# An encoder step on one core: the first token block's output projection, split into mixer B's heads and mixer A's heads

## The chip, the core and the metric

One core of a Trainium2 chip runs the whole layer. The figure compared is device time in microseconds (us) for one execution. Three runs of the kernel before took 2215.9, 2210.39 and 2213.52 us. The profile is of a further execution, which took 2217.6 us.

The engines are named as in the profile: PE multiplies matrices (PEld loads its stationary operand), DVE, ACT and POOL work elementwise, SP issues the DMAs. Each takes its own instructions in the order in which they are written for it, and waits for the others through semaphores.

## The reference

```python
def layer(x, c, ...):
    h = adaln_in(x, gains[0], sh1, sc1)
    x = x + FFN_RES * g1[:, None] * rmsnorm(swiglu(h, w1_gate, w1_up, w1_down), gains[1])
    h = adaln_in(x, gains[2], sh2, sc2)
    qa, ka, va, qb, kb, vb = jnp.split(h @ w_in, SPLITS, axis=-1)
    ...
    oa, ob, rows = mixers(qa, ka, va, qb, kb, vb)
    o = jnp.concatenate([rmsnorm(oa, group_gains[:WIDTH_A]), rmsnorm(ob, group_gains[WIDTH_A:])], axis=-1) @ w_out
    x = x + g2[:, None] * rmsnorm(o, gains[3])
    h = adaln_in(x, gains[4], sh3, sc3)
    x = x + FFN_RES * g3[:, None] * rmsnorm(swiglu(h, w2_gate, w2_up, w2_down), gains[5])
    return x, rows
```

There are 1024 prompt tokens and 32 new tokens; the model is 1024 wide. Mixer A is banded attention with 8 heads of 64 over up to 640 keys for each 128 queries, mixer B a narrow window with 8 query heads. Their outputs are 512 wide each. Each half is normalised by itself (a group norm), the two are joined to 1024 columns and multiplied by `w_out`.

## The kernel before

**Token blocks.** Everything but attention runs over three blocks of tokens, numbered tb: 384, 384 and 288 wide. Activations stand transposed, so a block's array is 8 slices k of 128 channels by its tokens. `O[tb]` (named `o` in the profile) holds attention's output: slices 0 to 3 are mixer A's four pairs of heads, 4 to 7 mixer B's.

**Two-part products.** A projection is computed from a rounded part and a rest of each operand: `mm3` issues three matmuls for each slice (weight high by `hi`, weight high by `lo`, weight low by `hi`). Weights are loaded as 128x1024 pieces (`raw`) and split by one ACT copy (L303) and one DVE subtraction (L304) into `w`.

**Attention.** It is a list of 72 tiles, gone through by the loop over n from L1275 on. Pair p of heads and query block i make a tile; tiles 0 to 35 are mixer B's, 36 to 53 pairs 0 and 1 of mixer A, and 54 to 71 pairs 2 and 3 in alternation, each pair beginning with its tile of the new tokens. A tile forms scores `S` (PE), adds the bias and finds the maximum (DVE), exponentiates (ACT), scales, transposes through `pp` (PE) to `PT`, and multiplies by the values into `po`, which is copied to `O`. Scores of tile n+1 are issued while tile n is transposed. The query and key projections (`pq`) fill PE up to n = 53; after that there are none left.

**The group norm** (L1138) of block tb and half g (0 is mixer A, 1 mixer B) squares two pieces of 128x768 on ACT (`sq`), adds them up on POOL, sums over channels by matmuls with ones (`pss`), computes a reciprocal root in ten small DVE operations (`rv`, `rt`, `ry`), spreads it over partitions by matmuls (`pr`), copies it (`rstd`, ACT), multiplies (`z`, DVE), rounds (`o_hi`, ACT) and takes the rest (`o_lo`, POOL for the first of two pieces and DVE for the second). It is a generator: `begin` puts it in a list of side work, `step` advances the first of that list by one piece, and `need` advances until one of them is finished.

**The order before.** At n = 55 (`GN1`) the mixer B norms of all three blocks begin. Mixer A's norm of a block begins two tiles after that block's last tile: n = 63 for block 0, n = 69 for block 1, and after the loop for block 2. `out_piece` (L1164) makes 128 output columns m of one block: 24 matmuls `wo`, then an ACT copy into `fo`. `OUTS` places five of block 0's eight pieces in the loop, one each at n = 67 to 71. The other three, then eight of block 1 (m from 7 down) and eight of block 2, follow the loop, with six side steps behind each. `KEEP` holds the weights of columns 5 to 7 from block 0 for block 1, so `w_out` is loaded in 13 pieces. After a block's last piece, its residual and next norm begin as side work (`h3`), which the second feed-forward (`gate`, `up`, `dn`) needs.

**Buffers.** 384-wide arrays of all kinds share six buffers (tag u): two are `O[0]` and `O[1]`, and the others hold the projections' inputs until n = 53. Scratch of 128x768 (`sq`, `z`, `PT` and others) shares five (tag h), raw weights three, split weights eight.

The program's order per engine comes from the framework's own scheduler, which moves instructions ahead of others where its estimate says that they are ready; so the written order is a priority, and the orders shown below are what was built.

Of the kernel before, what the change touches and what calls it, by code (L numbers as in the profile page):

```python
# [16 lines left out]
D = 1024  # L17
# [20 lines left out]
OUTSTEP = 6  # L38
ABREAST = 1
POOL_ADDS = (1, 2)  # L40
GN1 = 55
SC = (1, 3)
SCB = 1
JN = (1, 3)
# [21 lines left out]
PREP = 3  # L66
STAGES = ((0, 34), (37, 54))
RATE = 1.0
OUTS = (0,) * 13 + (1,) * 5
LAG = 0.5  # L70
KEEP = [(5, 6, 7), None, None]


@with_exitstack
def encoder_step(ctx: ExitStack, tc, x_prompt, x_sample, cache_a_k, cache_a_v, cache_b_k, cache_b_v,
# [30 lines left out]
    def s_tile(shape, name, dt=F32):  # L106
        return spool.tile(shape, dt, name=name, tag="s")
# [386 lines left out]
    def begin(key, gen, first=False):  # L494
        side.insert(0 if first else len(side), marked(key, gen))
# [641 lines left out]

    def group_norm(tb, g):  # L1138
        w = TB[tb][1]
        if OH[tb] is None:  # L1140
            OH[tb] = (u_tile(tb, "o_hi", F32R), u_tile(tb, "o_lo", F32R))
        hi, lo = OH[tb]
        pr = yield from mean_rstd(O[tb], range(4 * g, 4 * g + 4), w, 2.0 / D, JG, p1)
        r = s_tile([128, 384], "rstd")
        ae.activation(r[:, :w], pr[:, :w], AF.Copy)
        for c in range(2):
            z = h_tile([128, 2, 384], "z")
            for q in range(2):
                k = 4 * g + 2 * c + q
                ve.scalar_tensor_tensor(z[:, q, :w], O[tb][:, k, :], cst[:, 120 + k:121 + k], r[:, :w],  # L1150
                                        op0=OP.mult, op1=OP.mult)
            yield
            s = slice(4 * g + 2 * c, 4 * g + 2 * c + 2)
            ae.activation(hi[:, s, :], z[:, :, :w], AF.Copy)
            (ge if c in GNP else ve).tensor_tensor(lo[:, s, :], z[:, :, :w], hi[:, s, :], op=OP.subtract)
            yield

    wo, F2 = {}, [None] * 3
    outs = [(0, m) for m in range(KT)] + [(1, m) for m in reversed(range(KT))] + [(2, m) for m in range(KT)]

    def load_wo(m):
        wo[m] = split_cols(w_out, m)

    def out_piece():  # L1164
        tb, m = outs.pop(0)
# [67 lines left out]
    with tc.manual_schedule(engines={mybir.EngineType.PE}) if MANUAL else ExitStack():  # L1233
# [6 lines left out]
        for n in range(N):  # L1240
            for first, last, units in flows:
                if n == first:
                    now = now if PRIME == 2 and n == 0 else flow(units)
                    rate = sum(COST[key[0]] for key, _, _ in units) / (last - first) / 2 * RATE
            if n == GN1:
                for tb in range(3):
                    begin(("gn", tb, 1), group_norm(tb, 1))
            for tb in range(2):
                if n == whole[tb] + 2:
                    begin(("gn", tb, 0), group_norm(tb, 0), first=True)  # L1250
            for _ in range(OUTS[n - 54] if n >= 54 else 0):
                if outs and n >= whole[outs[0][0]] + 2:
                    out_piece()
            for key in opens.get(n + PREP, []):
                while key not in ready:
                    budget -= next(now, 0)
                preps.append(prepare(*key))
            for half in range(2):
                scores(n, half)
                tiles[n].tr(half)  # L1260
                if half == 0 and n:
                    tiles[n - 1].av()
                step(1)
                prep_step()
                fill(rate)
            for _, last, _ in flows:
                if n == last - 1:
                    fill(1e6)
                    budget = 0.0
    tiles[N - 1].av()  # L1270
    begin(("gn", 2, 0), group_norm(2, 0), first=True)
    while outs:
        out_piece()
# [82 lines left out]
```

## Time and profile before

| | |
|---|---|
| runs | 2215.9, 2210.39, 2213.52 us (median 2213.52) |
| profiled execution | 2217.6 us, of which the span from first to last instruction is 2215.8 us |
| DVE busy | 1239.1 us (56%) |
| ACT busy | 697.8 us (31%) |
| POOL busy | 179.2 us (8%) |
| mean granted PE clock | 0.984 |

A row of a window gives its start and end in us from the first instruction, its length, the busy time of each engine with the number of instructions, the granted share of PE's clock, the DMA engines' busy share and GB/s. A row of the timeline gives start, length, engine, line, operation and its operands; in brackets stands the engine's idle time before it and what ended it. PE's busy time is a model: matmuls overlap, so a start-to-start distance says more than a length.

### The profile page before, as it was taken

How to read it: one execution, taken by the hardware profiler on the slowest of the kernel's cores; microseconds unless marked ns; L12 is line 12 of the kernel's file. 1: busy time of each engine (PE TensorE's matmuls, PEld its weight loads, DVE VectorE, ACT ScalarE, POOL GpSimd, SP SyncE). 2: the span in 40 equal slices, each digit the busy share in tenths (PEclk: the TensorE clock that was granted, in tenths of full speed). 3: DMA queues.
4: the chain of work that ended last, by engine and by line, in shares of the span. 5: the costliest groups of instructions: out<-in, count | busy, mean ns of one | idle time of the engine just before them, and what ended most of it. 6: DMA issues, size and time to landing. Idle time of an engine off the chain costs nothing.

```text
span 2215.8 us, 33976 instructions
## 1 busy us (share of the span) xinstructions
PE 2161.6 (98%) x14012; PEld 2068.6 (93%) x14012; DVE 1239.1 (56%) x2425; ACT 697.8 (31%) x1450; POOL 179.2 (8%) x281
## 2 busy tenths in 40 slices
PE   6999999999999999899999899999999999999998
PEld 4999999999999999799787589999999999999998
DVE  5788667874333497677444865785333333333336
ACT  4411111111121253576444663542111111111133
POOL 1100000000000023001110313220000000000000
PEclk8999999999999999899999899999999999999999
DMA  9253334434122352111112121424211111111122
GB/s 323 93 153 118 111 96 124 143 101 129 39 66 69 101 184 93 38 39 30 50 30 62 46 77 67 134 86 120 66 58 39 57 39 39 58 38 58 39 69 79
DMA packets 200623, 186.03 MB, mean 84 GB/s; under 512 B 7597, under 2 KB 169813, under 8 KB 199317
## 3 DMA queue, kind: packets, MB, share of 16 engines
q1 hardware_dynamic: 200468, 183.87, 27.1%
q8 instruction: 110, 1.80, 0.3%
q14 instruction: 45, 0.36, 0.1%
HBM read 164.12 MB, written 22.86 MB: 84 GB/s over the span
## 4 chain that ended last, share of the span: by engine, by line
PE 90%; DVE 4%; DMA 3%; ACT 1%; issue 1%; POOL 0%; SPq 0%; ACTq 0%; DVEq 0%; POOLq 0%
PE dn L325 7%; PE dn L326 7%; PE dn L327 7%; PE gate L327 7%; PE gate L326 7%; PE up L327 7%; PE up L326 7%; PE gate L325 7%; PE up L325 7%; PE po L713 3%; PE S L752 2%; PE pq L325 2%; PE pq L327 2%; PE pq L326 2%; DMA raw<-in_w_gate_dram 1%; PE pp L776 1%
## 5 line engine op out<-in xcount | busy, mean ns | idle before, releaser
L326 PE MATMUL gate<-h_lo,w 128*128 128x384 f32 (+1 forms) x1056 | 340.2, 322 | 4.0 <-DVE h_lo L446 4.0
L325 PE MATMUL dn<-gg,w 128*128 128x384 f32 (+1 forms) x1056 | 341.4, 325 | 1.1 <-DVE facc L581 1.0
L581 DVE TENSOR_TENSOR facc<-dn,facc 128x768 f32<-128x768 f32 (+1 forms) x240 | 212.9, 889 | 230.2 <-PE dn L327 229.9
L326 PE MATMUL dn<-gg,w 128*128 128x384 f32 (+1 forms) x1056 | 340.6, 323 | 0.6 <-DVE gg L554 0.6
L325 PE MATMUL gate<-h_hi,w 128*128 128x384 f32 (+1 forms) x1056 | 341.0, 323 | 0.0
L327 PE MATMUL gate<-h_hi,w 128*128 128x384 f32 (+1 forms) x1056 | 340.4, 322 | 0.0
L325 PE MATMUL up<-h_hi,w 128*128 128x384 f32 (+1 forms) x1056 | 340.2, 322 | 0.0
L326 PE MATMUL up<-h_lo,w 128*128 128x384 f32 (+1 forms) x1056 | 340.0, 322 | 0.0
L327 PE MATMUL dn<-gg,w 128*128 128x384 f32 (+1 forms) x1056 | 340.0, 322 | 0.0
L327 PE MATMUL up<-h_hi,w 128*128 128x384 f32 (+1 forms) x1056 | 339.9, 322 | 0.0
L304 DVE TENSOR_TENSOR w<-raw,w 128x1024 fp32r<-128x1024 f32 x187 | 231.5, 1246 | 150.5 <-ACT w L303 150.3
L303 ACT ACTIVATE w<-raw 128x1024 fp32r<-128x1024 f32 x187 | 195.7, 1056 | 266.1 <-PE dn L327 103.5
L550 ACT ACTIVATE sl<-gate 128x384 f32<-128x384 f32 (+1 forms) x132 | 60.9, 462 | 563.9 <-PE gate L327 560.9
L551 DVE TENSOR_TENSOR sl<-sl,up 128x384 f32<-128x384 f32 (+1 forms) x132 | 68.5, 519 | 292.1 <-PE up L327 286.1
L326 PEld LDWEIGHTS gate<-h_lo,w 128*128 128x128 f32 x1056 | 198.6, 188 | 4.6 <-DVE h_lo L446 4.6
L325 PEld LDWEIGHTS dn<-gg,w 128*128 128x128 f32 x1056 | 199.2, 189 | 1.6 <-DVE facc L581 1.2
L326 PEld LDWEIGHTS dn<-gg,w 128*128 128x128 f32 x1056 | 199.2, 189 | 1.0 <-DVE gg L554 0.9
L327 PEld LDWEIGHTS dn<-gg,w 128*128 128x128 f32 x1056 | 199.1, 189 | 0.0
L325 PEld LDWEIGHTS gate<-h_hi,w 128*128 128x128 f32 x1056 | 198.7, 188 | 0.1
L327 PEld LDWEIGHTS gate<-h_hi,w 128*128 128x128 f32 x1056 | 198.7, 188 | 0.0
L327 PEld LDWEIGHTS up<-h_hi,w 128*128 128x128 f32 x1056 | 198.7, 188 | 0.0
L325 PEld LDWEIGHTS up<-h_hi,w 128*128 128x128 f32 x1056 | 198.5, 188 | 0.0
(224 smaller groups left out, 3367.4 us busy)
## 6 DMA issues: line engine op xcount, KB each, us to landing
raw<-in_w_mod_dram SPq DMA_DIRECT2D x56, 512.0 KB, 4.0
raw<-in_w_gate_dram SPq DMA_DIRECT2D x54, 512.0 KB, 4.0
raw<-in_w_up_dram SPq DMA_DIRECT2D x54, 512.0 KB, 4.7
raw<-in_w_down_dram SPq DMA_DIRECT2D x54, 512.0 KB, 4.5
raw<-in_w_in_dram SPq DMA_DIRECT2D x18, 512.0 KB, 4.3
wm<-in_w_mod_dram SPq DMA_DIRECT2D x8, 1024.0 KB, 7.4
raw<-in_w_out_dram SPq DMA_DIRECT2D x13, 512.0 KB, 4.5
xr<-xs SPq DMA_DIRECT2D x16, 384.0 KB, 3.5
```

The lines of the kernel that those rows point to most:

```text
L303: ae.activation(w[:, 0], r, AF.Copy)
L304: ve.tensor_sub(w[:, 1], r, w[:, 0])
L325: te.matmul(ps, w[:, 0, k], hi, start=start, stop=False)
L326: te.matmul(ps, w[:, 0, k], lo, start=False, stop=False)
L327: te.matmul(ps, w[:, 1, k], hi, start=False, stop=stop)
L550: ae.activation(sl[:, :w], ps[0][:, :w], AF.Silu)
L551: ve.tensor_tensor(sl[:, :w], sl[:, :w], ps[1][:, :w], op=OP.mult)
L581: ve.tensor_tensor(o, ps[:, :, :w], o, op=OP.add)
L713: te.matmul(po[64 * h:64 * h + 64, :n], vsl(j, h, kn), PT(h, j, kn), start=j == 0, stop=j == nt - 1)
L752: te.matmul(S[:, c:ce], self.T[:, h, :], KQ[:, 0, 128 * k0 + c:128 * k0 + ce], start=True, stop=True)
L776: te.transpose(pp[:, j - j0, :], P[:, 128 * j:128 * j + 128], ident)
```

## The change

Block 0's output projection is no longer made by `out_piece`. Each of its eight columns is made in two halves of the sum over channels: `half_piece` issues 12 matmuls over mixer B's four slices and copies the sum to `fo` (ACT); a later one issues 12 over mixer A's four slices and adds the sum to `fo` (DVE). The mixer B halves stand at n = 55 to 59, 61, 63 and 65; the mixer A halves at n = 66, 67 (one each) and 68 to 70 (two each). All of block 0 is so inside the loop, and after the loop 16 pieces follow where there were 19.

Each half loads its own weights, 512 rows by 256 columns for two halves: 8 pieces. Nothing is kept for block 1, which loads 8 pieces: 16 in all.

The norms move too. Block 0's mixer B norm begins at n = 51 and is finished by n = 54. The mixer B norms of blocks 2 and 1 begin at n = 65, in that order. A norm now asks for its output arrays after its reciprocal root and no longer before it.

```diff
-GN1 = 55
+GN1 = (51, 65)
+EARLY = (55, 56, 57, 58, 59, 61, 63, 65)
+LATE = 66
...
-OUTS = (0,) * 13 + (1,) * 5
...
-KEEP = [(5, 6, 7), None, None]
+KEEP = [None, None, None]
...
     def group_norm(tb, g):
         w = TB[tb][1]
+        pr = yield from mean_rstd(O[tb], range(4 * g, 4 * g + 4), w, 2.0 / D, JG, p1)
+        r = s_tile([128, 384], "rstd")
+        ae.activation(r[:, :w], pr[:, :w], AF.Copy)
         if OH[tb] is None:
             OH[tb] = (u_tile(tb, "o_hi", F32R), u_tile(tb, "o_lo", F32R))
         hi, lo = OH[tb]
-        pr = yield from mean_rstd(O[tb], range(4 * g, 4 * g + 4), w, 2.0 / D, JG, p1)
-        r = s_tile([128, 384], "rstd")
-        ae.activation(r[:, :w], pr[:, :w], AF.Copy)
...
-    outs = [(0, m) for m in range(KT)] + [(1, m) for m in reversed(range(KT))] + [(2, m) for m in range(KT)]
+    outs = [(1, m) for m in reversed(range(KT))] + [(2, m) for m in range(KT)]
...
+    halves = [(1, m) for m in range(KT)] + [(0, m) for m in range(KT)]
+    wh = {}
+
+    def load_half(g, j):
+
+        if (g, j) not in wh:
+            r = rpool.tile([128, 4, 256], F32, name="raw", tag="r")
+            dma.dma_start(r, w_out[0, 512 * g:512 * g + 512, 256 * j:256 * j + 256]
+                          .rearrange("(k p) n -> p k n", p=128))
+            w = wh[g, j] = wpool.tile([128, 2, 4, 256], F32R, name="w", tag="w")
+            ae.activation(w[:, 0], r, AF.Copy)
+            ve.tensor_sub(w[:, 1], r, w[:, 0])
+
+    def half_piece():
+
+        g, m = halves.pop(0)
+        need(("gn", 0, g))
+        if F2[0] is None:
+            F2[0] = u_tile(0, "fo", F32)
+        load_half(g, m // 2)
+        if m % 2 and halves:
+            load_half(halves[0][0], halves[0][1] // 2)
+        w, c0 = wh[g, m // 2], 128 * (m % 2)
+        hi, lo = OH[0]
+        ps = p1("wo")
+        for kk in range(4):
+            k = 4 * g + kk
+            wa, wb = w[:, 0, kk, c0:c0 + 128], w[:, 1, kk, c0:c0 + 128]
+            te.matmul(ps[:, :384], wa, hi[:, k, :], start=kk == 0, stop=False)
+            te.matmul(ps[:, :384], wb, hi[:, k, :], start=False, stop=False)
+            te.matmul(ps[:, :384], wa, lo[:, k, :], start=False, stop=kk == 3)
+        o = F2[0][:, m, :]
+        if g:
+            ae.activation(o, ps[:, :384], AF.Copy)
+        else:
+            ve.tensor_tensor(o, ps[:, :384], o, op=OP.add)
+        if m % 2:
+            del wh[g, m // 2]
+        if not halves:
+            begin(("h3", 0), between(F2[0], 0, 1, H3))
...
-            if n == GN1:
-                for tb in range(3):
-                    begin(("gn", tb, 1), group_norm(tb, 1))
+            if n == GN1[0]:
+                begin(("gn", 0, 1), group_norm(0, 1))
+            if n == GN1[1]:
+                begin(("gn", 2, 1), group_norm(2, 1))
+                begin(("gn", 1, 1), group_norm(1, 1))
...
-            for _ in range(OUTS[n - 54] if n >= 54 else 0):
-                if outs and n >= whole[outs[0][0]] + 2:
-                    out_piece()
+            if n == EARLY[0] - 1:
+                need(("gn", 0, 1))
+                load_half(1, 0)
...
                 fill(rate)
+                if half == 0 and n in EARLY:
+                    half_piece()
+                if n >= LATE and halves and (n + half) % 2 * (n < LATE + 2) == 0:
+                    half_piece()
...
     tiles[N - 1].av()
+    while halves:
+        half_piece()
+        step(2)
     begin(("gn", 2, 0), group_norm(2, 0), first=True)
```

**PE, at the start of the last two pairs.** Before, from the transposes of pair 3's tile of the new tokens (`pps`) on; the number behind a name tells tiles of one name apart:

```order
L902 MATMUL pps_11917<-ident_96,Ps_11872 128x64 x4
L903 MATMUL pps_11917<-ident_96,Ps_11872 32x64
L713 MATMUL po_11926<-PTs_11887,aux_11656 64x32 x8
L713 MATMUL po_11926<-PTs_11887,vs_9149 64x32 x2
L752 MATMUL S_12006<-KQ_11278,qz_11912 128x128
L776 MATMUL pp_11974<-ident_96,P_11908 128x128
L713 MATMUL po_11977<-PTs_11923,aux_11656 64x32 x8
L713 MATMUL po_11977<-PTs_11923,vs_9149 64x32 x2
L752 MATMUL S_12020<-KQ_10777,qz_11968 128x256
```

In the change, from the end of the first half piece to the start of the second:

```order
L1193 MATMUL wo_11987<-o_hi_11884,w_11908 128x384
L1194 MATMUL wo_11987<-o_hi_11884,w_11908 128x384
L1195 MATMUL wo_11987<-o_lo_11885,w_11908 128x384
L777 MATMUL pp_12027<-ident_96,P_11956 128x128
L753 MATMUL S_12061<-KQ_11278,qz_11960 128x128
L753 MATMUL S_12075<-KQ_10777,qz_12021 128x256
L714 MATMUL po_12030<-PTs_11971,aux_11660 64x32 x8
L714 MATMUL po_12030<-PTs_11971,vs_9149 64x32 x2
L1193 MATMUL wo_12047<-o_hi_11884,w_11908 128x384
L1194 MATMUL wo_12047<-o_hi_11884,w_11908 128x384
L1195 MATMUL wo_12047<-o_lo_11885,w_11908 128x384
```

Twelve `wo` matmuls in one run now stand between the scores and transposes of successive tiles.

**PE, at the end of the loop.** Before, the last matmul of attention (`po_13068`) stands among the pieces of block 0; from it to `pss_13111`, the sum of block 2's mixer A norm, are 19 `wo` of block 0's sixth piece, and behind `pr_13138` of that norm the seventh begins:

```order
L326 MATMUL wo_13085<-o_lo_11939,w_13082 128x384
L327 MATMUL wo_13085<-o_hi_11938,w_13082 128x384
L357 MATMUL pss_13111<-ones_98,sq_13115 128x1 x2
L357 MATMUL pss_13111<-ones_98,sq_13115 32x1
L405 MATMUL pr_13138<-ident_96,ry_13126 128x128 x2
L405 MATMUL pr_13138<-ident_96,ry_13126 128x32
L325 MATMUL wo_13147<-o_hi_11938,w_13144 128x384
L326 MATMUL wo_13147<-o_lo_11939,w_13144 128x384
```

In the change, from the last matmul of attention (`po_13159`) on; `pss_13171` and `pr_13198` belong to block 2's mixer A norm, `pss_13242` and `pr_13267` to block 1's mixer B norm, and `wo_13293` is block 1's first piece:

```order
L714 MATMUL po_13159<-PT_13145,vt_9148 64x128
L358 MATMUL pss_13171<-ones_98,sq_13175 128x1 x2
L358 MATMUL pss_13171<-ones_98,sq_13175 32x1
L406 MATMUL pr_13198<-ident_96,ry_13186 128x128 x2
L406 MATMUL pr_13198<-ident_96,ry_13186 128x32
L358 MATMUL pss_13242<-ones_98,sq_13246 128x1 x3
L406 MATMUL pr_13267<-ident_96,ry_13255 128x128 x3
L326 MATMUL wo_13293<-o_hi_13218,w_13290 128x384
L327 MATMUL wo_13293<-o_lo_13219,w_13290 128x384
```

No projection stands between attention's last matmul and the two norms any more.

**DVE, at the same place.** Before, from the last step of block 2's mixer A root on (`o_8219` is block 2's `O`, `o_8218` block 1's); the row behind these is the root of block 2's mixer B norm:

```order
L338 SCALAR_TENSOR_TENSOR ry_13126<-rt_13127,ry_13126 128x3
L1150 SCALAR_TENSOR_TENSOR z_13175<-o_8219,cst_110,rstd_13173 128x288 x2
L1150 SCALAR_TENSOR_TENSOR z_13180<-o_8219,cst_110,rstd_13173 128x288 x2
L1150 SCALAR_TENSOR_TENSOR z_13187<-o_8218,cst_110,rstd_13185 128x384 x2
L1150 SCALAR_TENSOR_TENSOR z_13223<-o_8218,cst_110,rstd_13185 128x384 x2
L1155 TENSOR_TENSOR o_lo_12792<-z_13180,o_hi_12791 128x576
L1155 TENSOR_TENSOR o_lo_12181<-z_13223,o_hi_12180 128x768
```

In the change, from the same step to the start of the root of block 1's mixer B norm (`rv_13253`):

```order
L339 SCALAR_TENSOR_TENSOR ry_13186<-rt_13187,ry_13186 128x3
L1151 SCALAR_TENSOR_TENSOR z_13206<-o_8219,cst_110,rstd_13202 128x288 x2
L1151 SCALAR_TENSOR_TENSOR z_13211<-o_8219,cst_110,rstd_13202 128x288 x2
L1151 SCALAR_TENSOR_TENSOR z_13220<-o_8218,cst_110,rstd_13216 128x384 x2
L1151 SCALAR_TENSOR_TENSOR z_13225<-o_8218,cst_110,rstd_13216 128x384 x2
L1151 SCALAR_TENSOR_TENSOR z_13232<-o_8219,cst_110,rstd_13230 128x288 x2
L1156 TENSOR_TENSOR o_lo_13205<-z_13211,o_hi_13204 128x576
L1151 SCALAR_TENSOR_TENSOR z_13237<-o_8219,cst_110,rstd_13230 128x288 x2
L1156 TENSOR_TENSOR o_lo_13219<-z_13225,o_hi_13218 128x768
L1156 TENSOR_TENSOR o_lo_13205<-z_13237,o_hi_13204 128x576
L392 TENSOR_SCALAR rv_13253<-pss_13242 128x3
```

Block 2's mixer B norm has moved in front of block 1's, whose whole chain now stands behind the loop. The square of block 1's mixer B half on ACT (`sq_13243`) stands behind the `o_hi` of `z_13232`, and POOL's additions of it behind three `o_lo`.

## The prediction

> **What bounds the kernel.** I read the page first, then windows over the stage around the change, then the timeline inside each window.
>
> ```profile
> PE 2161.6 (98%) x14012; PEld 2068.6 (93%) x14012; DVE 1239.1 (56%) x2425; ACT 697.8 (31%) x1450; POOL 179.2 (8%) x281
> PE 90%; DVE 4%; DMA 3%; ACT 1%; issue 1%; POOL 0%; SPq 0%; ACTq 0%; DVEq 0%; POOLq 0%
> ```
>
> PE is the bound, and the change removes no matmul of it. It can win only where PE lacks work or runs at a lower clock, and lose where its work leaves a gap uncovered. Three windows hold the places: from the last two pairs' start to the first exponential of tile 64, from there to the end of attention's last matmul, and 33 us behind it. The columns are PE, PEld, DVE, ACT, POOL, granted clock, DMA share and GB/s.
>
> ```profile
> 1213.00:1258.70 45.70, 39.36 (x235) 24.36 (x232) 36.56 (x105) 30.50 (x79) 19.14 (x51) 0.81 0.30 84
> 1258.70:1328.80 70.10, 69.44 (x495) 55.18 (x493) 49.77 (x125) 49.05 (x97) 14.67 (x22) 1.00 0.21 61
> 1328.80:1361.50 32.70, 29.53 (x158) 28.34 (x159) 19.64 (x42) 12.95 (x22) 13.75 (x10) 0.90 0.06 17
> ```
>
> In the first, PE idles 45.70 - 39.36 = 6.3 us, and a clock of 0.81 takes another 0.19 x 45.70 = 8.7 us. Short waits for softmax make it, such as
>
> ```profile
> 1224.83 0.33 PE L776 MATMUL pp<-ident,P 128*128 128x128 f32 x1 [1.48 <-ACT P L764]
> 1242.21 0.90 PE L776 MATMUL pp<-ident,P 128*128 128x128 f32 x3 [1.17 <-DVE P L766]
> ```
>
> The third holds the end of attention. PE's rows there:
>
> ```profile
> 1328.35 0.43 PE L713 MATMUL po<-PT,vt 128*64 128x128 f32 x2
> ...
> 1331.97 0.34 PE L327 MATMUL wo<-o_hi,w 128*128 128x384 f32 x1
> 1332.89 0.76 PE L357 MATMUL pss<-ones,sq 128*128 128x1 f32 x6 [0.58 <-POOL sq L370]
> 1336.01 1.76 PE L405 MATMUL pr<-ident,ry 128*128 128x128 f32 x6 [2.36 <-DVE ry L338]
> 1337.70 0.69 PE L325 MATMUL wo<-o_hi,w 128*128 128x384 f32 x1
> ...
> 1338.51 0.52 PE L327 MATMUL wo<-o_hi,w 128*128 128x384 f32 x1
> 1338.83 0.52 PE L325 MATMUL wo<-o_hi,w 128*128 128x384 f32 x1
> ...
> 1341.50 0.33 PE L325 MATMUL wo<-o_hi,w 128*128 128x384 f32 x1
> 1341.67 0.34 PE L326 MATMUL wo<-o_lo,w 128*128 128x384 f32 x1
> ```
>
> Attention's last matmul ends at 1328.8. PE then has 19 `wo` and two short waits, 2.9 us together. A `wo` starts 0.17 us after the one ahead at full clock (1341.50 to 1341.67) and 0.32 us at the low one (1338.51 to 1338.83), which lasts from 1337.7 to about 1341.
>
> **The change, part by part.** All sums use 0.174 us per `wo` at full clock.
>
> *Inside the loop.* Of the eight mixer B halves seven stand ahead of tile 64: 7 x 12 x 0.174 = 14.6 us into the first window, which has 6.3 + 8.7 = 15.0 us to spare, scattered in pieces shorter than a half's 2.1 us. PE takes them in written order, so a score or transpose behind a half waits for it, and DVE and ACT behind that score. In the second window the `wo` become fewer: nine halves, 108 matmuls, for
>
> ```profile
> 1258.70:1328.80 70.10, 23.66 (x126) 21.54 (x126) 2.45 (x5) 1.00 0.21 61
> ```
>
> so 18 x 0.174 = 3.1 us leave. DVE gains eight additions from PSUM and the loop three more weight splits; the nearest rows are
>
> ```profile
> L304 DVE TENSOR_TENSOR w<-raw,w 128x1024 fp32r<-128x1024 f32 x187 | 231.5, 1246 | 150.5 <-ACT w L303 150.3
> L303 ACT ACTIVATE w<-raw 128x1024 fp32r<-128x1024 f32 x187 | 195.7, 1056 | 266.1 <-PE dn L327 103.5
> L551 DVE TENSOR_TENSOR sl<-sl,up 128x384 f32<-128x384 f32 (+1 forms) x132 | 68.5, 519 | 292.1 <-PE up L327 286.1
> ```
>
> which makes 8 x 0.519 + 3 x 1.246 = 7.9 us on DVE and 3.2 on ACT. DVE was busy 36.56 + 49.77 = 86.3 of 115.8 us, 75%, and one norm's multiplications leave the loop, so most of this hides. Three more DMAs of 512 KB hide too (DMA share 0.30 and 0.21). The new order of the three matmuls of a product costs nothing, since every matmul has its own load already (14012 of each). Forcing block 0's mixer A norm at n = 66 puts its latency in front of a half; what PE waits for it has no row, and I leave it inside the bounds. Bounds: all idle time and the 3.1 us won, -9.4; all new DVE work exposed, +7.9. I take **-4**, on the gain's side because no engine but PE is above 75%.
>
> *At the loop's end.* This speaks against the change. Of block 0, 19 + 48 = 67 `wo` used to follow attention's last matmul; now none do, and block 1's first piece stands behind `pr` of two norms, one behind the other: block 2's mixer A, which needs attention's last output, and block 1's mixer B, whose operations DVE, ACT and POOL take behind those of three other norms. Queued behind that `pr` on PE are all 16 remaining pieces. The chain before, on the other engines:
>
> ```profile
> 1329.00 1.05 ACT L303 ACTIVATE w<-raw 128x1024 fp32r<-128x1024 f32 x1
> 1329.94 0.68 ACT L364 ACTIVATE sq<-o 128x576 f32<-128x576 f32 x1
> 1330.70 1.27 POOL L368 TENSOR_TENSOR sq<-sq 128x288 f32<-128x288 f32 x1 [3.23 <-ACT sq L364]
> 1337.81 0.79 ACT L1145 ACTIVATE rstd<-pr 128x288 f32<-128x288 f32 x2 [4.97 <-PE pr L405]
> 1338.25 5.09 DVE L1150 SCALAR_TENSOR_TENSOR z<-o,cst,rstd 128x288 f32<-128x288 f32 x8 [2.38 <-ACT rstd L1145]
> 1343.24 2.47 POOL L1155 TENSOR_TENSOR o_lo<-z,o_hi 128x768 fp32r<-128x768 f32 x1 [1.37 <-ACT o_hi L1154]
> 1354.39 2.31 ACT L364 ACTIVATE sq<-fo 128x768 f32<-128x768 f32 x3
> ```
>
> The changed order puts the same eight `z` at the same distance from attention's end, to 1343.3. What DVE and POOL do then, by form in the same stretch:
>
> ```profile
> L1150 DVE SCALAR_TENSOR_TENSOR z<-o,cst,rstd 128x288 f32<-128x288 f32 x8 | 5.1, 706 | 5.8 <-ACT rstd L1145 5.8
> L1155 POOL TENSOR_TENSOR o_lo<-z,o_hi 128x576 fp32r<-128x576 f32 x2 | 3.6, 1808 | 7.2 <-ACT o_hi L1154 7.2
> L1155 DVE TENSOR_TENSOR o_lo<-z,o_hi 128x576 fp32r<-128x576 f32 x2 | 2.7, 1365 | 0.0
> L368 POOL TENSOR_TENSOR sq<-sq 128x384 f32<-128x384 f32 x2 | 2.2, 1142 | 7.2 <-ACT sq L364 7.2
> L1155 DVE TENSOR_TENSOR o_lo<-z,o_hi 128x768 fp32r<-128x768 f32 x1 | 2.0, 2021 | 0.5 <-ACT o_hi L1154 0.5
> L1154 ACT ACTIVATE o_hi<-z 128x768 fp32r<-128x768 f32 x2 | 1.7, 840 | 1.5 <-DVE z L1150 1.5
> L370 POOL TENSOR_TENSOR sq<-sq 128x384 f32<-128x384 f32 x1 | 1.1, 1116 | 0.1
> ```
>
> DVE: four `z` (2.8), `o_lo` twice of 576 (2.7) and once of 768 (2.0), 7.6 us, to 1350.9. POOL: from its `o_lo`'s end at 1345.7 one more (1.8) and three additions (3.4), also to 1350.9. From a `pss` to the `wo` behind its `pr` took 4.8 us (1332.89 to 1337.70): PE restarts at 1355.7. Twelve `wo` over mixer A's slices at the low clock take 3.8 us; the next need mixer B's `o_hi`, behind a `rstd` and three squares on ACT (about 0.5 + 2.3 + 0.8 us, to 1359.4), and `o_lo` on POOL (2.5): 1361.9. The kernel before has by 1361.5 done
>
> ```profile
> 1328.80:1361.50 32.70, 25.69 (x134) 24.73 (x135) 2.41 (x5) 0.90 0.06 17
> ```
>
> 134 `wo`, 67 of which the change no longer owes. Of the other 67 the change has done 13. So it is 54 x 0.174 = 9.4 us behind, with the 0.4 us of the restart 9.8. If POOL and DVE did not slow each other (I allow 2 us), `pr` and the twelve `wo` ran at full clock (0.8 and 1.7), the restart would come 4.5 us earlier: +5.3. I take **+8**, near the rows of the same place. Behind the stall the low clock may last as it did before, ten `wo` at 0.15 us more: 0 to 1.5, I take **+0.7**. [...]
>
> *At the second feed-forward's start* block 1's norm is late:
>
> ```profile
> 1430.00:1450.00 20.00, 17.25 (x87) 16.78 (x86) 16.64 (x36) 8.51 (x15) 4.64 (x6) 0.83 0.10 35
> 1442.92 0.45 PE L326 MATMUL gate<-h_lo,w 128*128 128x384 f32 x1 [2.13 <-DVE h_lo L446]
> ```
>
> 2.75 us idle and 0.17 x 20 = 3.4 us of clock are lost. Block 0's residual and norm, which share DVE and ACT with block 1's, now come 28 `wo` (4.9 us) earlier against block 1's pieces (85 stand ahead of the residual's `pr`, and 113 did). Bounds -4.9 and +1 (a fifth of that, should DVE be late from the stall); I take **-2.5**.
>
> **The sum**: -4 + 8 + 0.7 - 2.5 = +2.2 us on the profiled execution's 2217.6 (span 2215.8), so 2219.8. That execution lies 4.1 us above the median of the runs, 2213.5; for the median the forecast is **2215.7 us**.
>
> **Rivals.**
>
> 1. *The stall is not paid back, slower.* If the halves delay scores as much as they fill, the loop keeps its length (0), the stall costs its upper 9.8, the clock 1.5, and the feed-forward gains nothing: +11.3, 2224.8 us. Its place is `pr` of block 1's mixer B norm. It decides as soon as the loop wins less than about 4 us. For it: every step of the chain has a row. Against: DVE and ACT have a quarter of the loop free.
> 2. *The loop shortens, faster.* The first window keeps its full clock and its waits are filled: -9.4, with +5.3, 0 and -4.9 for the rest: -9.0, 2204.5 us. For it: PE's loads are busy only 24.36 of 45.70 us there, so the busy 39.36 may hold waiting; the halves would then have 21.3 us to lie in. Against: the scores wait behind each half. [...]
> 3. *The halves don't fill the early gaps*, because weights or norm come late. The first `w_out` split was at 1217.1 (the row below), ahead of where the first half stands, so I give it little: the first two halves, 4.2 us, exposed, 2219.9 us.
>
> ```profile
> 1217.14 1.06 ACT L303 ACTIVATE w<-raw 128x1024 fp32r<-128x1024 f32 x1 [0.73 <-DMA raw<-in_w_out_dram]
> ```
>
> **How the numbers follow.** The likeliest case, a gain in the loop given back at its end, has 0.42 with its own range of 2208 to 2220; rival 1 has 0.30, rival 2 0.25 and rival 3 0.03. A measurement tells 0.3%, 6.6 us, from no change: faster lies below 2206.9 and slower above 2220.2. Rival 2 gives the 0.25, rival 1 and the upper edge of the likeliest 0.32, the rest 0.43. The range of 2204 to 2228 reaches to both rivals' times and a little past the first's, for the loop's +7.9 bound.
>
> **What would show it.** Right: 12 `wo` in a row between `pp` and `S` from about 1222 with a granted clock near 1.0 up to 1260; no `wo` for 20 us or more behind the last `po`, in it a wait of PE's second `pss` on POOL of some 13 us, and a further wait of 1 to 2 us at the first piece's thirteenth matmul. Wrong: a wait of less than 10 us there in all, or a loop that ends past 1333.

## The result, and the profile after

The changed kernel takes 2241.86 us (median of 4 runs, 2240.43 to 2243.28), the kernel before 2214.71 us (4 runs, 2210.39 to 2217.31). The ratio is 1.0123, with a 95% interval of 1.0111 to 1.0135: slower by 27 us, far outside the 2204 to 2228 that were forecast. The profiled execution after has a span of 2241.0 us against 2215.8, which is 25.2 us to explain. The first row of the page after, to be held against the one of before:

```profile
PE 2160.4 (96%) x14012; PEld 2069.8 (92%) x14012; DVE 1248.9 (56%) x2436; ACT 700.6 (31%) x1453; POOL 188.0 (8%) x281
```

PE has the same 14012 matmuls and the same busy time within 1.2 us (2161.6 before). What was added is time in which PE has nothing to do, and time at half clock. Windows of the trace after, cut at the same events as the prediction's three (the start of the last two pairs, the first exponential of tile 64, the end of attention's last matmul, 32.70 us behind it), and a fourth at the second feed-forward's start, which begins, like the prediction's, a microsecond or so ahead of the sums (`pss`) of block 1's norm; the columns are as there:

```profile
1213.57:1267.13 53.56, 47.04 (x310) 34.57 (x309) 36.98 (x89) 33.64 (x87) 20.60 (x49) 0.94 0.34 104
1267.13:1339.70 72.57, 70.36 (x486) 54.17 (x484) 51.42 (x137) 46.19 (x92) 14.07 (x23) 1.00 0.20 59
1339.70:1372.40 32.70, 9.33 (x35) 8.82 (x36) 20.81 (x43) 12.11 (x19) 13.43 (x10) 0.55 0.06 17
1446.00:1466.00 20.00, 15.73 (x74) 15.10 (x75) 11.70 (x31) 7.75 (x16) 2.94 (x4) 0.82 0.24 85
```

The first window has become 7.9 us longer and the second 2.5, so the loop 10.3 (forecast: 4 shorter). The loop holds 74 + 118 = 192 `wo` where before it held 126, and 66 x 0.174 = 11.5 us of work have thus moved into it (at full clock 13 `wo` started in 2.26 us before, from 1356.68 to 1358.94): it has won about 1 us. Idle time and low clock of the first window together were 15.0 us; now they are 53.56 - 47.04 + 0.06 x 53.56 = 9.7. All of that gain is the clock (8.7 to 3.2 us); the idle time is 6.5 us where it was 6.3.

**Where the first window lost.** PE, DVE and POOL after, where the two tiles of the new tokens stand:

```profile
1222.81 0.46 PE L903 MATMUL pps<-ident,Ps 64*128 64x64 f32 x4 [1.05 <-DVE Ps L893]
...
1229.16 0.69 PE L903 MATMUL pps<-ident,Ps 64*128 64x64 f32 x4 [3.64 <-DVE Ps L893]
1229.64 0.31 PE L904 MATMUL pps<-ident,Ps 64*32 64x64 f32 x1
1229.88 0.69 PE L1193 MATMUL wo<-o_hi,w 128*128 128x384 f32 x1
1230.37 0.52 PE L1194 MATMUL wo<-o_hi,w 128*128 128x384 f32 x1
```

```profile
1217.75 2.19 DVE L1151 SCALAR_TENSOR_TENSOR z<-o,cst,rstd 128x384 f32<-128x384 f32 x4
...
1220.77 1.98 DVE L893 TENSOR_SCALAR Ps<-Ps,den 64x544 f32<-64x544 f32 x1
...
1224.69 0.94 DVE L1156 TENSOR_TENSOR o_lo<-z,o_hi 128x768 fp32r<-128x768 f32 x1
1225.56 1.30 DVE L1176 TENSOR_TENSOR w<-raw,w 128x1024 fp32r<-128x1024 f32 x1
...
1228.44 0.67 DVE L893 TENSOR_SCALAR Ps<-Ps,den 64x544 f32<-64x544 f32 x1
```

```profile
1218.21 1.87 POOL L743 COPY qz<-KQ 64x128 f32<-64x128 f32 x1
...
1220.64 1.82 POOL L1156 TENSOR_TENSOR o_lo<-z,o_hi 128x768 fp32r<-128x768 f32 x1
```

The `z` and `o_lo` of block 0's mixer B norm, which the change puts here, stand on DVE among the softmax of the new-token tiles, beside three weight splits of the halves (1.2 to 1.3 us each, one of them shown). DVE is busy for 9.95 of the 10 us from 1219 to 1229; at the same place before, from 1214 to 1224, it was 8.33. `Ps` takes 1.98 us beside POOL's `o_lo`, where it took 0.49 before:

```profile
1215.51 0.49 DVE L892 TENSOR_SCALAR Ps<-Ps,den 64x544 f32<-64x544 f32 x1
```

PE waits 3.64 us for the second `Ps`; then the first half follows at half clock (granted 0.50 from 1226.75 to 1233.58), 0.32 us from `wo` to `wo` (1230.37 to 1230.69), and the scores of the next tile behind it.

**Behind the loop.** PE's rows after, all of them up to the first piece (the prediction shows those of before):

```profile
1338.38 1.31 PE L714 MATMUL po<-PT,vt 128*64 128x128 f32 x18
1343.77 1.21 PE L358 MATMUL pss<-ones,sq 128*128 128x1 f32 x6 [4.08 <-POOL sq L371]
1347.34 1.76 PE L406 MATMUL pr<-ident,ry 128*128 128x128 f32 x6 [2.37 <-DVE ry L339]
1363.82 1.44 PE L358 MATMUL pss<-ones,sq 128*128 128x1 f32 x6 [14.72 <-POOL sq L371]
1367.48 1.65 PE L406 MATMUL pr<-ident,ry 128*128 128x128 f32 x6 [2.22 <-DVE ry L339]
1368.78 0.67 PE L326 MATMUL wo<-o_hi,w 128*128 128x384 f32 x1
...
1373.40 0.41 PE L328 MATMUL wo<-o_hi,w 128*128 128x384 f32 x1
1373.65 0.34 PE L326 MATMUL wo<-o_hi,w 128*128 128x384 f32 x1
```

Between attention's last matmul (ended 1339.7) and the first `wo` lie 29.1 us with two `pss` and two `pr`. What the 14.72 us wait for, on DVE, ACT and POOL:

```profile
1349.58 7.51 DVE L1151 SCALAR_TENSOR_TENSOR z<-o,cst,rstd 128x288 f32<-128x288 f32 x10 [2.38 <-ACT rstd L1143]
```

```profile
1357.80 1.58 ACT L365 ACTIVATE sq<-o 128x768 f32<-128x768 f32 x2
```

```profile
1357.89 1.57 POOL L1156 TENSOR_TENSOR o_lo<-z,o_hi 128x576 fp32r<-128x576 f32 x1 [1.54 <-ACT o_hi L1155]
1359.42 2.88 POOL L369 TENSOR_TENSOR sq<-sq 128x384 f32<-128x384 f32 x2
1362.38 1.39 POOL L371 TENSOR_TENSOR sq<-sq 128x384 f32<-128x384 f32 x1
```

Ten `z` of three norms come first, then block 1's squares on ACT, then their additions on POOL behind its `o_lo`. That is the chain of the prediction.

### The profile page after: what moved, and what is told of

Read it like the earlier page. It is cut to its first block, busy times and chain, and to the rows that moved or that the text cites. A ratio compares the mean times of both kernels' runs of the same rounds, so it can differ in the third digit from the quotient of the medians.

```text
span 2241.0 us, 33985 instructions
## 1 busy us (share of the span) xinstructions
PE 2160.4 (96%) x14012; PEld 2069.8 (92%) x14012; DVE 1248.9 (56%) x2436; ACT 700.6 (31%) x1453; POOL 188.0 (8%) x281
## 3 DMA queue, kind: packets, MB, share of 16 engines
q1 hardware_dynamic: 199492, 185.44, 26.9%
## 4 chain that ended last, share of the span: by engine, by line
PE 89%; DVE 5%; DMA 3%; ACT 2%; issue 1%; POOL 0%; SPq 0%; ACTq 0%; DVEq 0%
PE gate L328 7%; PE dn L326 7%; PE gate L327 7%; PE dn L327 7%; PE up L326 7%; PE dn L328 7%; PE gate L326 7%; PE up L327 7%; PE up L328 7%; PE po L714 3%; PE S L753 2%; PE pq L326 2%; PE pq L328 2%; PE pq L327 2%; DMA raw<-in_w_gate_dram 1%; PE pp L777 1%
## 5 line engine op out<-in xcount | busy, mean ns | idle before, releaser
L305 DVE TENSOR_TENSOR w<-raw,w 128x1024 fp32r<-128x1024 f32 x182 | 226.6, 1253 | 140.3 <-ACT w L304 139.9
L304 ACT ACTIVATE w<-raw 128x1024 fp32r<-128x1024 f32 x182 | 190.5, 1056 | 271.7 <-PE dn L328 103.5
L326 PEld LDWEIGHTS dn<-gg,w 128*128 128x128 f32 x1056 | 197.8, 188 | 1.9 <-DVE facc L582 1.5
L327 PEld LDWEIGHTS dn<-gg,w 128*128 128x128 f32 x1056 | 198.3, 188 | 1.0 <-DVE gg L555 0.9
L327 PEld LDWEIGHTS up<-h_lo,w 128*128 128x128 f32 x1056 | 198.6, 188 | 0.0
```

The costliest lines, as they stand in the source:

```text
L304: ae.activation(w[:, 0], r, AF.Copy)
L305: ve.tensor_sub(w[:, 1], r, w[:, 0])
L326: te.matmul(ps, w[:, 0, k], hi, start=start, stop=False)
L327: te.matmul(ps, w[:, 0, k], lo, start=False, stop=False)
```

## The experiments

To compare the runs I cut each trace at the same five events: the 340th `po` from the last, which stands just ahead of the new-token tiles of the last two pairs, the first exponential of tile 64, the end of the last `po`, the first `gate` of the second feed-forward, and its 201st `dn`. A part's **loss** is its length less the length before, less 0.174 us for each `wo` that it holds more than before (plus 0.174 for each fewer). The norms' own matmuls are not corrected for, so a part that a norm has left gains them too. Ahead of the first and behind the last event together the kernels lie between 1.9 us below and 3.9 above the kernel before; the executions of one kernel lie as far apart (2210.39 to 2217.31 above). The ratios are to the kernel before as it was measured beside each run, with medians of 2214.7 to 2216.9 us. Lengths before: 54.8, 70.1, 85.4 and 133.9 us, with 0, 126, 450 and 0 `wo`.

| kernel | median, us | ratio to before, 95% interval | up to tile 64 | to the last `po` | to the first `gate` | to the 201st `dn` |
|---|---|---|---|---|---|---|
| the change | 2241.9 | 1.0123 [1.0111, 1.0135] | -5.1 | +3.9 | +22.4 | +3.1 |
| e1 norm early | 2237.1 | 1.0105 [1.0087, 1.0124] | -10.1 | +3.9 | +20.9 | +1.6 |
| e2 order | 2241.9 | 1.0124 [1.0105, 1.0144] | -5.1 | +4.0 | +33.6 | -8.4 |
| e3 cover | 2235.4 | 1.0096 [1.0079, 1.0113] | -5.1 | +5.5 | +14.3 | +0.5 |
| e4 split | 2218.8 | 1.0018 [1.0007, 1.0028] | -1.8 | +1.3 | +1.4 | +0.9 |
| e5 combo4 | 2229.9 | 1.0066 [1.0049, 1.0083] | -13.0 | +7.0 | +1.4 | +13.0 |
| e6 combo8 | 2215.2 | 1.0000 [0.9991, 1.0010] | -13.3 | +1.7 | +4.8 | +1.6 |
| e7 no pool | 2241.8 | 1.0117 [1.0102, 1.0132] | -4.5 | +3.9 | +22.0 | +0.6 |
| e8 shift | 2233.7 | 1.0077 [1.0062, 1.0092] | -14.5 | +6.1 | +21.9 | +0.5 |
| e11 b2 early | 2229.7 | 1.0057 [1.0042, 1.0072] | -2.9 | +4.1 | +10.2 | +2.1 |
| e9 late5 | 2207.5 | 0.9951 [0.9932, 0.9969] | -9.4 | -1.6 | +0.3 | 0.0 |
| e10 cover6 | 2217.3 | 1.0005 [0.9995, 1.0014] | -7.3 | +6.0 | +2.9 | +0.3 |
| e12 late6 | 2207.2 | 0.9961 [0.9948, 0.9973] | -9.1 | -2.1 | +2.1 | -5.0 |

The first row reads: 5.1 us were won up to tile 64, 3.9 lost in the rest of the loop, 22.4 behind it and 3.1 at the second feed-forward's start, 24.3 of the 25.2. The last row's profile is of its fastest run, 2201.5, some 6 us below its median, and that of e10 is of its slowest, 2223.4, some 6 us above.

**e1. Block 0's mixer B norm earlier.**

```
-GN1 = (51, 65)
+GN1 = (45, 65)
```

> The changed kernel with one number changed: block 0's mixer B norm starts at n = 45 in place of 51, so its four z, its two o_lo and its squares lie ahead of the two new-token tiles and no longer among their Ps. Theory A (the loop's loss of 8 us at 1221 to 1235 is that norm's work on DVE and POOL among the new-token tiles): PE's 3.6 us wait of pps for Ps goes, tile 64's first exponential comes 4 to 8 us earlier, 2234 to 2238 us. Theory B (the loss there is the halves' four weight splits of 1.2 us each on DVE): nothing changes, 2240 to 2243. Theory C (the loss is at the loop's end alone): nothing changes in the total either, 2240 to 2243, and tile 64's first exponential may move without effect.

Measured 2237.1 us. PE's waits in this run between 1195 and 1390 (us in total, times, longest):

```profile
PE pss L358 <- POOL sq L371: 18.8, 2, 14.7
...
PE pps L903 <- DVE Ps L893: 0.4, 1, 0.4
```

The wait for `Ps` has fallen from 4.7 us in two to 0.4, the part up to tile 64 is 5.0 us shorter, and the total 4.8. Theory A holds for that much; B falls, since the four weight splits stayed. The 14.7 us behind the loop are untouched.

**e7. The same norm without POOL.**

```
-            (ge if c in GNP else ve).tensor_tensor(lo[:, s, :], z[:, :, :w], hi[:, s, :], op=OP.subtract)
+            (ge if c in GNP and (tb, g) != (0, 1) else ve).tensor_tensor(lo[:, s, :], z[:, :, :w], hi[:, s, :], op=OP.subtract)
```

> The changed kernel with both o_lo of block 0's mixer B norm on DVE, none on POOL; the norm stays at n = 51. If POOL and DVE slow each other among the new-token tiles (qz 1.9 us where it took 0.28, Ps 1.98 where it took 0.49), the pps wait of 3.6 us falls below 1.5, and the time by 2 to 4 us, 2238 to 2240. If DVE's own queue is the cause, it gets 0.95 us more: 2241 to 2244, the wait as long or longer.

Measured 2241.8 us: nothing. In this run DVE's `Ps` is fast again, and PE waits elsewhere; DVE, PE and ACT:

```profile
1222.03 0.49 DVE L893 TENSOR_SCALAR Ps<-Ps,den 64x544 f32<-64x544 f32 x1
```

```profile
1222.58 0.46 PE L903 MATMUL pps<-ident,Ps 64*128 64x64 f32 x4 [0.28 <-DVE Ps L893]
1222.88 0.22 PE L904 MATMUL pps<-ident,Ps 64*32 64x64 f32 x1
1226.55 0.66 PE L714 MATMUL po<-PTs,aux 128*64 128x32 f32 x16 [3.45 <-ACT PTs L706]
```

```profile
1225.17 1.06 ACT L1175 ACTIVATE w<-raw 128x1024 fp32r<-128x1024 f32 x1 [1.84 <-DMA raw<-in_w_out_dram]
1226.13 0.46 ACT L706 ACTIVATE PTs<-pps 128x256 f32<-128x256 f32 x2
```

`Ps` came in time, but ACT evacuates its transposes behind a weight split that itself waits 1.84 us for its DMA. In the change these two stand the other way round on ACT, `PTs` at 1223.41 and the split at 1224.83: with the edit the scheduler has changed ACT's order as well, and DVE has 0.94 us more of `o_lo` to do. So this run shows that the slowing of `Ps` by POOL can be taken away, and not what it cost; that stays open. The time is that of the second alternative and the fallen wait that of the first; neither had named ACT.

**e8. Besides e1, the mixer B halves from tile 57.**

```
-EARLY = (55, 56, 57, 58, 59, 61, 63, 65)
+EARLY = (57, 58, 59, 60, 61, 62, 63, 65)
```

> The early norm (n = 45) of the first run, and besides the mixer B halves from tile 57 in place of 55, so that none lies among the new-token tiles; end as in the changed kernel. If the rest of the first window's loss is the first halves at half clock among the new-token tiles (12 wo at 0.32 us): 2 to 4 us below the first run's 2237.1, 2233 to 2235. If the halves fill there as well as behind: 2236 to 2239.

Measured 2233.7 us, 3.3 below e1, and 14.5 us won up to tile 64. PE in e1, with the last `wo` of the first half and the scores around it, and then in e8:

```profile
1220.99 0.46 PE L753 MATMUL S<-KQ,qz 128*128 128x128 f32 x2 [0.55 <-ACT Ps L889]
...
1227.16 0.52 PE L1195 MATMUL wo<-o_lo,w 128*128 128x384 f32 x1
1227.48 1.05 PE L753 MATMUL S<-KQ,qz 128*128 128x128 f32 x4
```

```profile
1222.17 0.81 PE L753 MATMUL S<-KQ,qz 128*128 128x128 f32 x4 [0.49 <-ACT Ps L889]
...
1225.15 1.10 PE L753 MATMUL S<-KQ,qz 128*128 128x128 f32 x4
```

The four scores behind the half in e1 stand 22.4 us behind the first event (1205.1). In e8 two of them are the last of its first row, and the other two the first of its second, at 16.1 and 18.8 us (from 1206.4). In e1 all twelve `wo` of the first half run at 0.32 us, in e8 five of them, which is 7 x 0.15 = 1.0 us; the rest I put down to the softmax that no longer stands behind a half. Half of the 4.4 us won there is lost again in the rest of the loop (+3.9 to +6.1).

**e4. The halves alone, at the places of the whole pieces.**

```
-halves = [(1, m) for m in range(KT)] + [(0, m) for m in range(KT)]
+halves = [(g, m) for m in range(KT) for g in (0, 1)]
...
+            if n >= LATE + 1 and n >= whole[0] + 2:
+                half_piece()
+                half_piece()
```

with the norms begun as before and no half's weights loaded ahead.

> The halves alone: block 0's projection in the same 16 half sums with their eight additions on DVE, but the two halves of a column back to back at the places where the kernel before has its whole pieces, with the norms begun as before (all three mixer B norms at n = 55). No prefetch of a half's weights. If the split itself (8 more evacuations of 0.52 us, a half's weights by 512 KB) costs what is missing: 2220 to 2230. If only the places do (theories A and C): 2211 to 2218.

Measured 2218.8 us, ratio 1.0018: the split costs some 4 us of the 27 (1.6 to 6.2 by the interval), just above the bound I had set for "places only". The rest is the places of the halves and of the norms, which this run puts back together.

**e3. Four mixer A halves left behind the loop.**

```
-                if n >= LATE and halves and (n + half) % 2 * (n < LATE + 2) == 0:
+                if n >= LATE and len(halves) > 4 and (n + half) % 2 * (n < LATE + 2) == 0:
```

> The changed kernel with the last four mixer A halves left behind the loop: 48 wo, 8.4 us at full clock, stand between attention's last matmul and the pss of the norms. Theory C (PE is without work there for want of cover, and the loop was lengthened by the halves' own matmuls): the loop ends 6 to 8 us earlier, the four halves run in what was idle, 2233 to 2236. Rival (the loop's end is set by softmax's latency on ACT and DVE, and not by PE): the loop ends less than 3 us earlier and the restart comes as late behind the loop plus the halves, 2240 to 2246.

Measured 2235.4 us, 6.4 below the change, as theory C had it. The loop is 6.6 us shorter, and the longest wait for POOL's additions is 6.6 us where it was 14.7; PE's waits:

```profile
PE pss L358 <- POOL sq L371: 8.1, 2, 6.6
PE pr L406 <- DVE ry L339: 6.2, 2, 3.9
```

**e2. Block 1's norms ahead of block 2's.**

```
-                begin(("gn", 2, 1), group_norm(2, 1))
                 begin(("gn", 1, 1), group_norm(1, 1))
+                begin(("gn", 2, 1), group_norm(2, 1))
...
-    begin(("gn", 2, 0), group_norm(2, 0), first=True)
+    begin(("gn", 2, 0), group_norm(2, 0))
```

> The changed kernel with block 1's mixer B norm begun ahead of block 2's, and block 2's mixer A norm begun behind block 1's instead of ahead of it: block 1's first piece no longer stands behind the pr of block 2's mixer A norm. Theory C (what was lost behind attention's last matmul is the chain of norms in front of block 1's first piece): the first wo comes 5 to 12 us behind attention's last matmul instead of 29, and the time falls by 12 to 20 us, 2222 to 2230. Rival (DVE, ACT and POOL owe the same norms whatever the order, so the stall moves behind block 1's pieces or into the loop): less than 4 us, 2238 to 2243.

Measured 2241.9 us, no change: the rival was right. PE in this run, behind the loop's end (1340.7) and ahead of block 2's first piece:

```profile
1343.33 0.44 PE L326 MATMUL wo<-o_hi,w 128*128 128x384 f32 x1 [2.61 <-ACT o_hi L1155]
...
1406.04 1.21 PE L358 MATMUL pss<-ones,sq 128*128 128x1 f32 x6 [10.03 <-POOL sq L371]
1409.53 1.79 PE L406 MATMUL pr<-ident,ry 128*128 128x128 f32 x6 [2.27 <-DVE ry L339]
1414.58 1.09 PE L326 MATMUL wo<-o_hi,w 128*128 128x288 f32 x3 [3.27 <-ACT o_hi L1155]
```

The first `wo` comes 2.6 us behind attention, as theory C wanted, and the stall stands 55 us behind the loop's end, in front of block 2's pieces, whose mixer A norm now waits behind block 0's residual and norm. Behind the loop and at the feed-forward together, e2 loses 25.2 us and the change 25.5.

**e11. Block 2's mixer B norm in the loop.**

```
-            if n == GN1[1]:
+            if n == GN1[2]:
                 begin(("gn", 2, 1), group_norm(2, 1))
+            if n == GN1[1]:
                 begin(("gn", 1, 1), group_norm(1, 1))
```

with `GN1 = (51, 65, 58)`.

> The changed kernel with one norm moved: block 2's mixer B norm starts at n = 58 in place of 65, inside the loop; block 1's mixer B norm still starts at n = 65 and now gets the last tiles' steps. One norm chain (block 2's mixer A) then stands between attention's last matmul and block 1's first piece, not two. If the stall is the chain of two norms one behind the other: the wait of 14.7 us for POOL goes, the first wo comes 8 to 16 us behind attention's last matmul in place of 29, 2222 to 2232 us. If the norms' work only stands elsewhere (as when block 2's norms went behind block 1's, where the same time was lost between the pieces): 2236 to 2243.

Measured 2229.7 us, 12.2 below the change. PE behind the loop (attention ends at 1340.2):

```profile
1344.28 1.21 PE L358 MATMUL pss<-ones,sq 128*128 128x1 f32 x6 [4.08 <-POOL sq L371]
1347.85 1.75 PE L406 MATMUL pr<-ident,ry 128*128 128x128 f32 x6 [2.37 <-DVE ry L339]
1355.02 1.33 PE L326 MATMUL wo<-o_hi,w 128*128 128x384 f32 x3 [5.42 <-ACT o_hi L1155]
```

One norm chain instead of two, 14.8 us to the first `wo` instead of 29.1, and the loss there falls from 22.4 to 10.2. This norm reads only mixer B's heads of block 2 and writes buffers of its own, so nothing had kept it at n = 65; the kernel before begins it at n = 55.

**e5 and e6. The gains together.** Both: block 0's mixer B norm from n = 45, from n = 66 block 1's mixer B norm ahead of block 2's, block 2's mixer A norm queued behind block 1's and ahead of block 0's residual. e5 has four mixer A halves behind the loop; e6 has all eight there and the mixer B halves from tile 57.

> The edits of the two runs that gained, together, and an order of the norms that takes up what the second run showed: block 0's mixer B norm from n = 45; from n = 66 block 1's mixer B norm ahead of block 2's; four mixer A halves behind the loop; block 2's mixer A norm behind block 1's norms, but now ahead of block 0's residual and norm. If the early norm (4.8 us) and the cover (6.4 us) add and block 1's first piece finds its norms done: 2241.9 - 11.2 = 2230.7, less the 8 to 14 us that the stall still had with cover alone, 2214 to 2224 us, with no wait of more than 5 us of PE between attention's last matmul and the second feed-forward. If the stall only moves behind block 1's pieces, as in the run with the order alone: 2228 to 2234, with a wait of 8 us or more for POOL or DVE there.

> As the run before, with all eight mixer A halves behind the loop (96 wo, 16.7 us at full clock) and the mixer B halves from tile 57 on, two tiles behind the new-token tiles. If cover is what the loop's end lacks, the loop ends 6 us or more earlier than with four left and the time is 0 to 8 us below that run's, down to 2208; the gain of the change itself (7.5 us of idle time filled in the first window) should then show against the kernel before. If the loop has as much idle time at its end as the halves need, the halves do better inside it: 2 to 6 us above that run's.

Measured 2229.9 and 2215.2 us. In e5 the stall behind the loop is gone (+1.4), and 13.0 us are lost at the second feed-forward's start instead, where PE waits for `gg`, `h_lo` and `h_hi` (3.7, 2.8 and 1.4 us). The time is that of my second case, by other waits than I had named. With cover for twice as long, e6 loses little anywhere behind the loop and is level with the kernel before, 14.7 us below e5, more than I had expected.

**e9, e10 and e12. What each had shown, in one kernel.** All: block 0's mixer B norm from n = 45, halves from tile 57, block 2's mixer B norm from n = 58, block 1's from n = 66, three steps of the norms for each half behind the loop. They differ in the mixer A halves:

```
 e9   LATE = 69   len(halves) > 5     tiles 69 to 71, five behind the loop
 e10  LATE = 66   len(halves) > 6     tiles 66 and 67, six behind the loop
 e12  LATE = 70   len(halves) > 6     tiles 70 and 71, six behind the loop
```

> All that gained so far in one kernel: block 0's mixer B norm from n = 45, the mixer B halves from tile 57, block 2's mixer B norm from n = 58, block 1's from 66, three mixer A halves beside the last three tiles and five behind the loop, three steps of the norms for each, block 2's mixer A norm ahead of block 0's residual. Against the run with all eight behind the loop (2215.2) one norm fewer stands behind the loop, so block 0's residual and norm come about 7 us earlier and the second feed-forward's start should not wait, and the last tiles' waits (some 4 us from 1298 to 1313) get work: 2203 to 2211. If what is won there is lost to DVE and POOL beside the pairs' tiles: 2213 to 2220.

> As the run before, but with two mixer A halves beside tiles 66 and 67 and six behind the loop: if the place of the halves in the loop's last tiles does not matter, within 3 us of that run; if the last three tiles are where PE lacks work, 2 to 5 us above it.

> The last kernel with one number changed: the two mixer A halves of the loop stand beside tiles 70 and 71 in place of 66 and 67; six stay behind the loop, as there. If PE is full at tiles 66 and 67 and lacks work only in the last two or three tiles (some 8 us of waiting there), so that a half costs its own 2.1 us at the one place and nothing at the other: 5 to 10 us below that kernel's 2217.3, 2207 to 2212. If it is the number of halves behind the loop that decides (five there gave 2207.5): 2215 to 2219.

Measured 2207.5, 2217.3 and 2207.2 us. e9 and e12 are faster than the kernel before by 0.5 and 0.4%, with intervals that do not reach 1. The two longest waits of PE in e9 from 1195 to 1480 are

```profile
PE pr L406 <- DVE ry L339: 3.3, 1, 3.3
PE gate L327 <- DVE h_lo L447: 2.2, 1, 2.2
```

and no stall like those above is left. e10 and e12 differ in one number, and by 10 us. The last 40 us of the loop in each:

```profile
1290.60:1330.60 40.00, 36.47 (x262) 26.25 (x258) 28.79 (x78) 27.98 (x57) 9.05 (x7) 0.96 0.21 60
```

```profile
1274.50:1314.50 40.00, 39.56 (x308) 30.25 (x305) 31.36 (x83) 31.72 (x67) 10.97 (x12) 1.00 0.18 54
```

With the halves at tiles 70 and 71 (second row) PE lacks 0.4 us and keeps its clock, with them at 66 and 67 it lacks 3.5 us, most of it in one wait for a norm's sum:

```profile
1321.46 0.83 PE L358 MATMUL pss<-ones,sq 128*128 128x1 f32 x6 [2.27 <-POOL sq L371]
```

So the loop's last tiles have room for the two halves. At 66 a half also needs block 0's mixer A norm, which is pulled forward for it; no wait of PE shows what that costs (none at the two halves there, from 1294 to 1306, is longer than 0.6 us).

## Why the prediction was wrong

**The loop, forecast -4, measured +10.3.** This is the step that failed, and 14.3 of the 23 us between the forecast's +2.2 and the profile's +25.2. It put "14.6 us into the first window, which has 6.3 + 8.7 = 15.0 us to spare" and said of what DVE and ACT get that "most of this hides". Most of the room was there: in e8 the part up to tile 64 wins 14.5 us, some 11 of them idle time and low clock (some 15 us before, some 4 in e8); that part of e8 also holds 18 matmuls of norms fewer. The change wins 5.1 of the 14.5. 5.0 go to the norm's work among the new-token tiles (e1), 4.4 to the halves among them (e8). I had looked at the average of DVE over the stage, 75%, and not at the ten us in which the two new-token tiles stand: there it was busy 8.33 us already, and with the norm's work its rows are back to back (9.95). In the rest of the loop, where PE had 0.66 us idle, I counted 3.1 us as leaving with 18 `wo` fewer. It was 8 fewer, and 3.9 us were lost beside them. e10 against e12 shows that the places of the mixer A halves matter there: their profiles differ by 8.1 us in this part (+6.0 and -2.1), though these two executions lie on opposite sides of their medians, which are 10 us apart in all. The pulled-forward norm, which I left "inside the bounds", comes with them, and the two were not separated. My bound of +7.9 was wrong in kind: it priced the worst case by DVE's new operations and left out that 66 `wo` which fill no gap bring their own 11.5 us.

**The end of the loop, forecast +8 and +0.7, measured +10.9** (the 22.4 of the table less the 11.5 us of `wo` that left). The mechanism was right, piece by piece: two `pr` one behind the other, 14.7 us of waiting at the second `pss` (forecast some 13), the first `wo` 29.1 us behind attention (26.9). e11 and e3 show it by taking away one norm and by giving cover. Only the size was low. The chain to the first `wo` took 2.2 us more than I had added up. The further wait at the thirteenth matmul did not come. The low clock lasted 15 `wo`, 15 x 0.15 = 2.2 us. My 0.7 is not all that I had for it: the restart behind the +8 has twelve `wo` at 0.32 us, another 1.7. No single figure is right here: behind the same 29.1 us without `wo` the low clock lasted 5 `wo` in e1, 13 in e7 and 12 in e8.

**The second feed-forward's start, forecast -2.5, measured +3.1.** The row of the fourth window has 4.3 us idle and a clock of 0.82, where 2.75 and 0.83 were. The gain did not come: `pr` of block 1's norm stands 22.4 us behind the first `gate`, and it stood 22.3 behind it before. How much is lost is less firm: with the same order of the norms e1, e3, e7 and e8 lose 1.6, 0.5, 0.6 and 0.5 us there, and 1.7 of the change's 3.1 is low clock that those four do not have (5.1 against 3.4 us, by the granted clock). Block 0's residual stands fewer `wo` ahead of block 1's pieces, as I said, but behind a stall in which it did not run. That the stall causes it is argued, not shown: no run moves this term alone. e2 (-8.4) and e5 (+13.0) change the order of the norms in the queue and with it this part; but e9, e10 and e12 also have block 2's mixer A norm ahead of block 0's residual, as e5 has, and lose 0.0, +0.3 and -5.0, so that order alone does not decide it.

**The split itself,** forecast as hidden: e4 bounds it at some 4 us, with its weights not loaded ahead.

**The rivals.** The first, "the stall is not paid back", had the right side and the right place behind the loop, and its 2224.8 us were 17 too low, 10.3 of them because it held the loop's length at 0 and 3.1 at the feed-forward. The second did not come about. It took the 21.3 us in which PE's loads were not busy (24.36 of 45.70) for room. No run here decides between that and the 15.0 of idle time and clock: the most `wo` that any run has up to tile 64 are the 81 of e11, 14.1 us.

**The signs I had named:** the loop ended past 1333, at 1339.7, which was a sign of being wrong; the stall and the wait of the second `pss` were signs of being right, and came. The twelve `wo` in a row came, at 1229.9 and not 1222, and the clock of the first window was 0.94. The third rival, that early halves don't fill, had 0.03 and was in part what happened, though its reason was another: the first half stood behind `Ps`, not behind late weights or a late norm.

## What to carry to other kernels

Price matmuls that are moved into a full stage at their whole time first (here 66 `wo`, 11.5 us, and the loop grew by 10.3), and then subtract only those gaps whose neighbours on the other engines have rows free at that very place, not on the average of a stage. Before work that covers a chain of norms is moved away, count the chains that it covered: one of them here cost 12 us of PE, and another order only moved the loss, while moving that norm to where it had long been possible won it back. A stall that vanishes from its place has to be looked for behind the next pieces before it counts as won.

## What the runs showed of the hardware

Short operations of DVE and POOL took longer beside long ones of the other: `Ps` of 64x544 on DVE took 1.98 us beside POOL's `o_lo` and 0.49 without it (in the kernel before and in e7), and POOL's copy of 64x128 took 1.87 us (from 1218.21) beside DVE's four `z` (1217.75 to 1219.94), where it takes

```profile
1209.18 0.28 POOL L742 COPY qz<-KQ 64x128 f32<-64x128 f32 x1
```

in the kernel before. POOL's `o_lo` ran from 1220.64 to 1222.46, and `Ps`, started at 1220.77, ended 0.29 us after it. Why they stretch, no run here shows. e7, which took this away from `Ps`, gained nothing, but it changed ACT's order too, so the price of the stretching is open.

How long the half clock lasted behind a stall was not fixed here. In the changed kernel the granted clock was 0.50 from 1342.81 to 1373.53, and the `wo` stand 0.32 us apart for 4.6 us from the first one on (1368.78 to 1373.40); behind the same 29.1 us it was 1.4 us in e1, 4.0 in e7 and 3.7 in e8. In the record of the changed kernel the stretches in which half the clock was granted last 3.41, 6.83, 10.24 and 30.72 us, in that of the kernel before 3.41, 6.83 and 10.24, whole multiples of 3.41 us, but for the last one of each, which the end of the record cuts off. By an estimate from these (half of 3.41) the low clock's cost to a part so came in steps of about 1.7 us, and I do not count one such step between single profiles as a difference of two kernels.
